# Retuned scheduling preferences in the mixing of a hybrid RWKV-7 and attention layer

## The chip, the cores and the metric

The kernel runs on one core of a Trainium2 chip. A core has five engines with instruction queues of their own: TensorE (PE, matrix products), VectorE (DVE), ScalarE (ACT), GpSimd (POOL) and SyncE (SP), which here does nothing but issue DMAs. Each engine works through its instructions strictly in order; across engines they wait for each other by semaphores. The metric is the time of one execution on the device, in microseconds.

## The reference

One layer of a streaming encoder, for 16 meta tokens, 512 tokens of a prompt and 64 tokens of a sample (592 rows of 1024 values):

```python
x += 1/2 * SwiGLU_a(RMSNorm(x))
p  = RMSNorm(x) @ w_in              # RWKV: r, k, v, decay, a, gate;  MLA: q-latent, kv-latent, rope-key
o_rwkv = RWKV-7 time mixing         # 8 heads of 64, a state per head, delta rule per token
o_mla  = latent attention           # 8 heads, causal by chunks of 64
x += concat(o_rwkv, o_mla) @ w_out
x += 1/2 * SwiGLU_b(RMSNorm(x))     # d_ff 2816
y  = RMSNorm(x)
```

RWKV's recurrence, per head and token, is `S = S*w + (S @ -kk) * kka + v * k` and `y = S @ r`. The kernel computes it in chunks of 64 tokens, for which a unit triangular system has to be solved in each chunk. Everything is float32; the large products are formed from split operands in three passes.

## The kernel before

The time has three stages: the first feed-forward network (to about 400 us), the mixing (to about 890 us), and the second feed-forward network. The change concerns the mixing.

**Units of RWKV.** `rwkv_unit(i, h, s)` treats head pair i (0 to 3) and half h of the tokens (0, 1): unit `3_0` is pair 3, first half. It is a generator with pauses (`yield`). Its first part prepares the chunk's operands and ends with the matrix `am` (L761), whose lower triangles go to DRAM as `ud` (four stores, L773) and come back as `up` (four loads, L777) with another layout. The second part turns operands by transposes (`tp`, `tb`, L791 and L792). Then comes the *solve*: `qm` is loaded with unit rows (L825), and 31 pairs of operations on POOL, `tt` (L830) and `qm` (L832), 62 steps in all, eliminate one column after the other; the result is stored as `qd` (L834) and read back into `qt` (four loads, L838). All of these DMAs are issued by SP (`RQ = nc.sync`). The rest of the unit forms the chunk's state products (`xb` L851 and L860, `tw` L875, `mps` L896, `sp` L918, `yp` L938 and on).

**Attention.** `attention(i)` treats two heads (pair i): keys and values from the latent (`kp` L1077, `vp` L1087), queries (`qp`, L1101), then nine blocks: four query tiles t of 128 rows for each of two heads hh, and one of the sample. `P_2_1_0` is pair 2, tile 1, head 0. For a block, scores `s` (L1155) go to PSUM, `softmax` fills the tile P, whose padding behind the last key is first set to zero by POOL (L1110; P has two buffers), and PE transposes P in blocks of 128 keys (`ptp`, L1134). The last of these blocks contains the zeroed columns. The products with the values are `ao` (L1186), and they go to DRAM as `od` (L985) or straight into the operands of the output product `wo` (L161 to L163).

**What sets the order.** The program is written as units and attention steps in turn (the loop at the end of the functions below). A scheduler then puts the instructions of each engine in an order by priorities and its own estimate of times. `later(what)` shifts the priority of everything that is issued inside it by `PRIORITY[what]` (or by the entry of the name's first part, such as `F2` for `F2_1`). `ATTENTION[n] = (before, during, after)` says how many steps of attention are issued ahead of, between and behind the later parts of unit n. So both tables hold numbers alone, and both decide in which place of each engine's queue an instruction stands.

Of the kernel before, what the change touches and what calls it, by code (L numbers as in the profile page):

```python
# [35 lines left out]
BANK_ORDER = ("C", "A", "D", "A", "D", "D", "B", "C")  # L36


PRIORITY = {"B": -1300, "S": -1600, "F2": -2400, "F1": -1300, "att": 1100, "w": 19300, "W": -500, "S_3": -3100,
# [6 lines left out]
ATTENTION = ((10, 0, 5), (11, 0, 4), (13, 0, 5), (13, 0, 7), (15, 0, 4), (12, 0, 7), (8, 0, 1), (11, 1, 13))  # L46


START = {"f1": "0aaaaaaa0aaa0babbbbbb0bbbb000110011t1t1121t212t222222", "f2": "aa0aaaaaba0ba1bb0babb0babb00b001101t1t1121t212t222222"}
# [31 lines left out]
def build(ctx: ExitStack, tc: tile.TileContext, I, O):  # L81
# [492 lines left out]
    @contextmanager  # L574
    def later(what):

        p, d = tc.cur_priority, PRIORITY.get(what, PRIORITY.get(what.split("_")[0], 0))
        tc.cur_priority = p + d
        yield
        tc.cur_priority -= d  # L580
# [619 lines left out]
    for n in range(8):  # L1200
        before, during, after = ATTENTION[n]
        with later(f"S_{n}"):
# [163 lines left out]
```

## Time and profile before

| | |
|---|---|
| median of 3 runs | 1304.87 us (1303.28 to 1307.77) |
| profiled execution | 1302.65 us |
| its span, first to last instruction | 1300.5 us |
| mean granted clock of PE | 0.983 |
| PE busy | 1259.3 us, 97% of the span |
| DVE, ACT, POOL busy | 990.7, 597.0, 545.0 us |

The profiled execution is one execution of its own, 2.22 us below the median; the times of rows come from it. A granted clock of 1.00 means 2.4 GHz, 0.50 means 1.2 GHz. In a timeline, a row gives the start, the duration (of all instructions of the row, where "x4" stands behind it), the engine, the line, and what was written from what; in brackets, how long the engine had been idle and what it waited for. SPq rows are DMA issues: the time is that of issuing, not of the transfer.

### The profile page before, as it was taken

What the parts mean: (1) busy time and instruction counts of PE and PEld (TensorE: products, weight loads), DVE (VectorE), ACT (ScalarE), POOL (GpSimd) and SP (SyncE); (2) the same over time, 40 slices, a digit from 0 to 9 for tenths busy, and PEclk for the clock granted to TensorE, in tenths of its full rate; (3) what the DMA queues carried; (4) which work ended last, traced back from release to release, by engine and by line L of the source; (5) the groups of instructions that cost most, each with busy time, mean ns of one, the idle gap of its engine ahead of it and who ended that gap; (6) DMA issues with size and microseconds to landing.
All of it is one profiled execution on the core that took longest, in us unless ns stands there. A gap on an engine that the chain in (4) does not pass through costs nothing. (4 is left out here: it accounts for less than half of the span.)

```text
span 1300.5 us, 26629 instructions
## 1 busy us (share of the span) xinstructions
PE 1259.3 (97%) x10104; PEld 1172.7 (90%) x10104; DVE 990.7 (76%) x2044; ACT 597.0 (46%) x1326; POOL 545.0 (42%) x811
## 2 busy tenths in 40 slices
PE   8999999999999999999999999998999999999997
PEld 7999999999999988877776667888999999999997
DVE  7876979888886654667677765578967989898974
ACT  7442434343444555554564545446533434343442
POOL 2333637464671006464562663000013736374760
PEclk9999999999999998989998989999999999999999
DMA  8222232323103422212113111134222222323112
GB/s 288 81 83 73 80 103 71 98 85 110 41 22 123 137 82 66 69 49 61 42 49 114 40 38 49 32 116 147 99 74 74 95 84 82 104 76 98 49 35 73
DMA packets 84255, 107.02 MB, mean 82 GB/s; under 512 B 24160, under 2 KB 44832, under 8 KB 84128
## 3 DMA queue, kind: packets, MB, share of 16 engines
q1 hardware_dynamic: 84128, 105.33, 26.3%
q8 instruction: 80, 1.31, 0.4%
q14 instruction: 47, 0.39, 0.1%
HBM read 96.78 MB, written 8.52 MB: 81 GB/s over the span
## 5 line engine op out<-in xcount | busy, mean ns | idle before, releaser
L830 POOL TENSOR_TENSOR tt<-qm,up 80x60 f32<-80x60 f32 (+24 forms) x248 | 84.9, 343 | 49.3 <-DMA up<-ud 21.3
L832 POOL TENSOR_TENSOR qm<-qm,tt 80x60 f32<-80x60 f32 (+24 forms) x248 | 84.0, 339 | 18.5
L1110 POOL MEMSET P<- 128x112 f32 (+1 forms) x36 | 6.8, 192 | 126.9 <-PE ptp L1134 87.6
L461 DVE SCALAR_TENSOR_TENSOR x<-f2o,x 128x288 f32<-128x288 f32 x88 | 38.7, 453 | 25.9 <-PE f2o L163 25.9
L461 DVE SCALAR_TENSOR_TENSOR x<-f1o,x 128x296 f32<-128x296 f32 x88 | 39.5, 461 | 23.6 <-PE f1o L163 23.5
L137 POOL TENSOR_TENSOR n_ops<-n,n_ops 128x296 fp32r<-128x296 f32 (+1 forms) x8 | 7.6, 948 | 90.9 <-DMA f_3A<-in_w13b 67.6
L161 PE MATMUL wo<-o,wo_h 128*128 128x288 f32 x128 | 41.2, 328 | 2.0 <-DVE x L1017 1.3
L162 PE MATMUL wo<-o,wo_h 128*128 128x288 f32 x128 | 39.8, 312 | 0.0
L163 PE MATMUL wo<-o,wo_l 128*128 128x288 f32 x128 | 38.0, 299 | 0.0
L136 ACT CAST f1w_h<-f1w_r 128x512 fp32r<-128x512 f32 x32 | 19.5, 617 | 21.8 <-PE f1o L162 19.8
L161 PEld LDWEIGHTS wo<-o,wo_h 128*128 128x128 f32 x128 | 24.0, 189 | 5.3 <-DVE x L1017 2.5
L1155 PE MATMUL s<-keys,qh 128*128 128x264 f32 (+3 forms) x80 | 27.9, 444 | 0.9 <-ACT pt L1140 0.5
L136 ACT CAST f2w_h<-f2w_r 128x512 fp32r<-128x512 f32 x32 | 19.2, 616 | 18.7 <-PE f2o L162 16.7
L761 DVE TENSOR_TENSOR am<-ab,cst 128x512 f32<-128x512 f32 (+1 forms) x32 | 15.0, 484 | 16.6 <-PE ab L757 16.5
L1134 PE MATMUL ptp<-ident,P 128*128 128x128 f32 (+1 forms) x128 | 23.2, 292 | 3.7 <-DVE P L1124 1.5
L1017 DVE TENSOR_TENSOR x<-wo,x 128x288 f32<-128x288 f32 x48 | 21.7, 454 | 6.7 <-PE wo L163 6.3
L1118 ACT ACTIVATE P<-s,m 128x264 f32<-128x264 f32 (+3 forms) x40 | 19.2, 483 | 15.9 <-DVE m L1116 15.6
L162 PEld LDWEIGHTS wo<-o,wo_h 128*128 128x128 f32 x128 | 24.3, 190 | 1.3 <-issue 0.7
L1134 PEld LDWEIGHTS ptp<-ident,P 128*128 128x128 f32 (+1 forms) x128 | 15.0, 144 | 11.1 <-issue 4.3
L163 PEld LDWEIGHTS wo<-o,wo_l 128*128 128x128 f32 x128 | 24.2, 189 | 0.8
L137 DVE TENSOR_TENSOR f1w_l<-f1w_r,f1w_h 128x512 fp32r<-128x512 f32 x32 | 24.0, 751 | 1.1 <-ACT f1w_h L136 0.2
L716 POOL MEMSET e<- 128x5 f32 x8 | 0.8, 106 | 56.9 <-DVE bk L765 56.9
(1261 smaller groups left out, 5677.0 us busy)
## 6 DMA issues: line engine op xcount, KB each, us to landing
f1w_r<-in_w2a SPq DMA_DIRECT2D x40, 256.0 KB
f2w_r<-in_w2b SPq DMA_DIRECT2D x40, 256.0 KB
wo_r<-in_w_out SPq DMA_DIRECT2D x12, 256.0 KB
up<-ud SPq DMA_DIRECT2D x32, 80.0 KB
x<-in_xT SPq DMA_DIRECT2D x8, 296.0 KB
xd<-x SPq DMA_DIRECT2D x2, 1184.0 KB
x<-xd SPq DMA_DIRECT2D x2, 1152.0 KB
f_1A<-in_w13a SPq DMA_DIRECT2D x4, 512.0 KB
```

What stands on the lines that cost most here:

```text
L136: S.copy(dst_hi, src)
L137: sub.tensor_tensor(dst_lo, src, dst_hi.bitcast(F32), ALU.subtract)
L161: T.matmul(out, wh, xh, start=i == 0, stop=False)
L162: T.matmul(out, wh, xl, start=False, stop=False)
L163: T.matmul(out, wl, xh, start=False, stop=i == n - 1)
L461: V.scalar_tensor_tensor(x[h][:, m], o[:, :n], 0.5, x[h][:, m], ALU.mult, ALU.add)
L830: G.tensor_tensor(t3, qm[:, :nj, st:st + 1].to_broadcast([4 * NP, nj, w]), up[:, st:st + 1, st + 1:].to_broadcast([4 * NP, nj, w]), ALU.mult)
L832: G.tensor_tensor(qm[:, :nj, st + 1:], qm[:, :nj, st + 1:], t3, ALU.subtract)
L1017: V.tensor_tensor(x2s[h][:, m], ps[:, :n], x2s[h][:, m], ALU.add)
L1118: S.activation(P[:, p0:p0 + n], s[:, :n], AF.Exp, bias=m[:, 2:3], scale=SCALE, accum_out=m[:, 4 + j:5 + j])
L1134: T.transpose(tp[:an, 128 * k:128 * k + 128], P[:, a0:a0 + an], ident)
L1155: T.matmul(s[:, :an], Q[:, hh, q0:q0 + 128], K[:, hh, a0:a0 + an], start=True, stop=True)
```

## The change

Numbers in the two tables change, and five names get an entry of their own. The same instructions are issued; the engines' queues differ between 574 us and 892 us of the trace of before, and are the same ahead of and behind that. In the changed kernel every line stands one further down, since the table has one line more.

```diff
-PRIORITY = {"B": -1300, "S": -1600, "F2": -2400, ...
+PRIORITY = {"B": -1300, "S": -1600, "F2": -2000, ...
...
-            "F1_7": -300, "W_k3": -800, "F2_7": -2600, "F1_0": -1200, "B_6": -1500, "W_k1": 700}
-ATTENTION = ((10, 0, 5), (11, 0, 4), (13, 0, 5), (13, 0, 7), (15, 0, 4), (12, 0, 7), (8, 0, 1), (11, 1, 13))
+            "F1_7": -300, "W_k3": -800, "F2_7": -2600, "F1_0": -1200, "B_6": -1500, "W_k1": 700, "F2_1": -4000,
+            "att_3": 200, "B_7": -2500, "B_4": -100, "S_5": -1200}
+ATTENTION = ((10, 0, 5), (11, 0, 4), (13, 0, 7), (13, 0, 8), (15, 0, 4), (12, 0, 8), (8, 0, 1), (11, 1, 13))
```

**SP, where unit 2_1's solve ends and unit 3_0's begins.** Before, the queue holds (`ud` and `up` feed the solve of 3_0, `qd` and `qt1` carry the result of 2_1; `wq3` are weights of attention):

```order
L773 DMA ud_3_0_9221<-am_3_0_9201 32x5x32 x4
L834 DMA qd_2_1_9659<-qm_2_1_9564 80x8x32
L1097 DMA wq3_0_10091<-in_wq 128x256
L777 DMA up_3_0_9226<-ud_3_0_9221 20x1024 x4
L838 DMA qt1_5279<-qd_2_1_9659 32x5x32 x4
L825 DMA qm_3_0_10437<-in_rows 80x256
```

In the changed kernel:

```order
L986 DMA od_5255<-ot_5_384_8816 128x128
L835 DMA qd_2_1_9692<-qm_2_1_9597 80x8x32
L986 DMA od_5255<-xn_1_1_8945 128x320
L839 DMA qt1_5279<-qd_2_1_9692 32x5x32 x4
L826 DMA qm_3_0_10460<-in_rows 80x256
L986 DMA od_5255<-ot_5_512_9041 128x64
L774 DMA ud_3_0_9247<-am_3_0_9227 32x5x32 x4
L778 DMA up_3_0_9252<-ud_3_0_9247 20x1024 x4
```

The store `qd` and the loads `qt1` of unit 2_1 have moved ahead of `ud` and `up` of unit 3_0, and so has one store of attention.

**POOL, at the start of unit 3_0's solve.** Before, from the last steps of unit 2_1's solve on:

```order
L832 TENSOR_TENSOR qm_2_1_9564<-qm_2_1_9564,tt_2_1_29_9653 80x8x2
L830 TENSOR_TENSOR tt_2_1_30_9656<-qm_2_1_9564,up_2_1_8421 80x8
L832 TENSOR_TENSOR qm_2_1_9564<-qm_2_1_9564,tt_2_1_30_9656 80x8
L716 MEMSET e_3_1_9678 128x5
L1110 MEMSET P_2_1_0_9314 128x112
L1110 MEMSET P_2_1_1_9332 128x112
L830 TENSOR_TENSOR tt_3_0_0_10439<-qm_3_0_10437,up_3_0_9226 80x31
L832 TENSOR_TENSOR qm_3_0_10437<-qm_3_0_10437,tt_3_0_0_10439 80x31
L830 TENSOR_TENSOR tt_3_0_1_10442<-qm_3_0_10437,up_3_0_9226 80x30
```

In the changed kernel, from the fourth step of unit 3_0's solve on:

```order
L833 TENSOR_TENSOR qm_3_0_10460<-qm_3_0_10460,tt_3_0_1_10465 80x30
L831 TENSOR_TENSOR tt_3_0_2_10468<-qm_3_0_10460,up_3_0_9252 80x29
L833 TENSOR_TENSOR qm_3_0_10460<-qm_3_0_10460,tt_3_0_2_10468 80x29
L831 TENSOR_TENSOR tt_3_0_3_10471<-qm_3_0_10460,up_3_0_9252 80x28
L833 TENSOR_TENSOR qm_3_0_10460<-qm_3_0_10460,tt_3_0_3_10471 80x28
L831 TENSOR_TENSOR tt_3_0_4_10474<-qm_3_0_10460,up_3_0_9252 80x54
L833 TENSOR_TENSOR qm_3_0_10460<-qm_3_0_10460,tt_3_0_4_10474 80x2x27
L831 TENSOR_TENSOR tt_3_0_5_10477<-qm_3_0_10460,up_3_0_9252 80x52
L833 TENSOR_TENSOR qm_3_0_10460<-qm_3_0_10460,tt_3_0_5_10477 80x2x26
L1111 MEMSET P_2_1_0_9314 128x112
```

The zeroing of P_2_1_0 has moved from in front of the solve to behind its twelfth step. That of P_2_1_1 follows after the twentieth. The transposes `ptp` of P_2_1_0 stand at the same place of PE's work in both kernels.

**PE, where attention pair 3 and the output product begin.** Before (`kp` and `vp` are keys and values of pair 3, `wo_0_1` and `wo_0_0` parts of the output product):

```order
L1077 MATMUL kp_3_424_10073<-cT_5631,w_uk_3_10065 128x424
L1087 MATMUL vp_3_0_10078<-w_uv_3_10066,cT_5631 128x128 x4
L161 MATMUL wo_0_1_0_10185<-o0_10132,wo_0_0_h_10166 128x288
L162 MATMUL wo_0_1_0_10185<-o0_10132,wo_0_0_h_10166 128x288
L163 MATMUL wo_0_1_0_10185<-o0_10132,wo_0_0_l_10167 128x288
L1087 MATMUL vp_3_4_10084<-w_uv_3_10066,cT_5631 128x128 x2
L1087 MATMUL vp_3_4_10084<-w_uv_3_10066,cT_5631 80x128
L634 MATMUL yp_2_1_9977<-acc_2_1_10012,cst_5262 128x320
```

In the changed kernel `kp_3_424` stands six rows ahead of these:

```order
L162 MATMUL wo_0_0_0_10194<-o0_10155,wo_0_0_h_10189 128x288
L792 MATMUL tp_3_0_4_10057<-ident_67,rkv_3_0_9183 128x128
L793 MATMUL tp_3_0_4_10057<-ident_67,bk_3_0_9184 128x128
L163 MATMUL wo_0_0_0_10194<-o0_10155,wo_0_0_h_10189 128x288
L164 MATMUL wo_0_0_0_10194<-o0_10155,wo_0_0_l_10190 128x288
L809 MATMUL av_3_0_10065<-zt_3_0_10040,am_3_0_9227 64x64 x8
L625 MATMUL yp_2_1_9996<-acc_2_1_10021,cst_5262 10x64 x5
L818 MATMUL gb_3_0_10079<-sga_5265,w_g2_3_8520 128x320
L809 MATMUL av_3_0_10065<-zt_3_0_10040,am_3_0_9227 64x64 x2
L1088 MATMUL vp_3_4_10084<-w_uv_3_9873,cT_5631 128x128 x2
L1088 MATMUL vp_3_4_10084<-w_uv_3_9873,cT_5631 80x128
```

The second part of the values, `vp_3_4`, has moved away from `kp_3_424`, and the products `wo_0` and the transposes of unit 3_0 stand between them.

## Rows read from the trace of the kernel before

**Rows 1.** the page: busy time, share and instructions of each engine:
```profile
PE 1259.3 (97%) x10104; PEld 1172.7 (90%) x10104; DVE 990.7 (76%) x2044; ACT 597.0 (46%) x1326; POOL 545.0 (42%) x811
```

**Rows 2.** table of windows: length; busy PE, PEld, DVE, ACT, POOL (count); clock, DMA share, GB/s:
```profile
574.00:892.00 318.00, 302.79 (x3026) 237.55 (x3027) 221.11 (x689) 169.90 (x459) 125.08 (x400) 0.97 0.24 69
```

**Rows 3.** PE's waits from 574 to 892 us: total, times, longest:
```profile
PE wo L161 <- DVE x L1017: 1.3, 1, 1.3
...
PE tp L791 <- ACT zt L801: 1.2, 2, 0.8
...
PE vp L1087 <- ACT keys L1079: 1.1, 1, 1.1
...
PE wo L161 <- ACT o L136: 0.7, 1, 0.7
```

**Rows 4.** timeline of POOL, 735 to 745 us: start, duration, what, idle before:
```profile
735.28 0.19 POOL L1110 MEMSET P<- 128x112 f32 x1 [4.45 <-PE ptp L1134]
...
737.55 0.23 POOL L830 TENSOR_TENSOR tt<-qm,up 80x31 f32<-80x31 f32 x1 [1.40 <-DMA qm<-in_rows]
...
742.03 0.27 POOL L830 TENSOR_TENSOR tt<-qm,up 80x50 f32<-80x50 f32 x1
...
744.86 0.31 POOL L832 TENSOR_TENSOR qm<-qm,tt 80x66 f32<-80x66 f32 x1
```

**Rows 5.** timeline of PE: transposes of P_2_1_0, then of P_2_1_1:
```profile
741.02 0.55 PE L1134 MATMUL ptp<-ident,P 128*128 128x128 f32 x3
...
744.82 0.38 PE L1134 MATMUL ptp<-ident,P 128*128 128x128 f32 x2
```

**Rows 6.** timeline of SP's DMA issues, 726 to 738 us:
```profile
727.04 1.77 SPq L773 DMA_DIRECT2D ud<-am  x4
730.83 0.30 SPq L834 DMA_DIRECT2D qd<-qm  x1
...
731.89 1.66 SPq L777 DMA_DIRECT2D up<-ud  x4
733.60 1.84 SPq L838 DMA_DIRECT2D qt<-qd  x4
735.49 0.43 SPq L825 DMA_DIRECT2D qm<-in_rows  x1
```

**Rows 7.** timeline of SP: unit 2_0's ud, up, qd and qt; unit 2_1's ud and up:
```profile
640.81 1.81 SPq L773 DMA_DIRECT2D ud<-am  x4
643.90 1.41 SPq L777 DMA_DIRECT2D up<-ud  x4
...
674.50 0.34 SPq L834 DMA_DIRECT2D qd<-qm  x1
676.45 1.77 SPq L838 DMA_DIRECT2D qt<-qd  x4
...
692.36 2.04 SPq L773 DMA_DIRECT2D ud<-am  x4
699.25 1.60 SPq L777 DMA_DIRECT2D up<-ud  x4
```

**Rows 8.** timeline of POOL: first step of the solve behind up at 643.90:
```profile
647.78 0.23 POOL L830 TENSOR_TENSOR tt<-qm,up 80x31 f32<-80x31 f32 x1 [5.45 <-DMA up<-ud]
```

**Rows 9.** windows around three half-speed stretches; columns as in rows 2:
```profile
693.47:696.88 3.41, 1.75 (x39) 1.52 (x40) 2.14 (x14) 3.27 (x12) 0.01 (x1) 1.00 1.09 360
696.88:703.71 6.83, 6.83 (x70) 4.93 (x68) 3.00 (x9) 0.97 (x5) 0.59 (x3) 0.50 0.35 92
...
754.90:765.14 10.24, 9.86 (x78) 7.22 (x78) 6.50 (x20) 2.95 (x11) 5.54 (x21) 0.50 0.21 48
...
789.04:792.45 3.41, 3.41 (x10) 2.54 (x8) 2.43 (x6) 1.29 (x4) 2.63 (x11) 0.50 0.31 91
```

**Rows 10.** timelines of SP and PE: unit 3_0's qd, and its first xb:
```profile
762.65 0.30 SPq L834 DMA_DIRECT2D qd<-qm  x1
...
792.66 0.50 PE L851 MATMUL xb<-q,am 32*32 32x32 f32 x20
```

More of the change, by code (lines that the diff above doesn't have):

```diff
@@ L36 @@
 BANK_ORDER = ("C", "A", "D", "A", "D", "D", "B", "C")
-PRIORITY = {"B": -1300, "S": -1600, "F2": -2400, "F1": -1300, "att": 1100, "w": 19300, "W": -500, "S_3": -3100,
[6 rows of a table removed]
-ATTENTION = ((10, 0, 5), (11, 0, 4), (13, 0, 5), (13, 0, 7), (15, 0, 4), (12, 0, 7), (8, 0, 1), (11, 1, 13))
+PRIORITY = {"B": -1300, "S": -1600, "F2": -2000, "F1": -1300, "att": 1100, "w": 19300, "W": -500, "S_3": -3100,
[7 rows of a table added]
+ATTENTION = ((10, 0, 5), (11, 0, 4), (13, 0, 7), (13, 0, 8), (15, 0, 4), (12, 0, 8), (8, 0, 1), (11, 1, 13))
 START = {"f1": "0aaaaaaa0aaa0babbbbbb0bbbb000110011t1t1121t212t222222", "f2": "aa0aaaaaba0ba1bb0babb0babb00b001101t1t1121t212t222222"}
```

10 rows, old and new, of the table PRIORITY are left out of this document.

## The prediction

> **What bounds the kernel now.** I read the page first. TensorE (PE) is busy 97% of the span [rows 1]; so time is lost only where PE waits, or where its clock is halved. The order of every engine is the same in both kernels up to 574 us and from 892 us on, so the change acts only in the 318 us of the mixing between them. The table of windows says that PE is busy 302.79 us of these at a mean clock of 0.97 [rows 2]: 15.2 us of idle time is all that a better order could win there, apart from the clock. The list of PE's waits in that stretch shows this idle time as some thirty listed waits of 0.2 to 1.3 us; rows 3 are the ones that the argument needs [rows 3]. No single one carries the kernel; what a new order can do to the end is to take some of them away, or to make a long one.
>
> For a long one I looked at what runs beside PE with little room. GpSimd (POOL) works through the triangular solve of one RWKV unit in 62 steps, in order, and between them zeroes the padding of attention's P tiles. The solve of unit 3_0 starts at 737.55, and the P tile of block 1_0 of attention pair 2 (P_2_1_0) is zeroed ahead of it, at 735.28 [rows 4]. PE transposes this tile with the row at 741.02 [rows 5], so the zeroing has 6 us to spare before the change. SyncE (SP) issues every DMA in order; the loads and stores that feed the solve stand in its queue [rows 6].
>
> **The change part by part.** It moves instructions and neither adds nor removes one, so engine time is the same and only waits count.
>
> 1. *The zeroing of P.* In the changed kernel P_2_1_0 is zeroed after 12 steps of the solve of 3_0 instead of before the solve. PE's transposes of that tile stand at the same place in PE's work as before. So PE now waits for the start of this solve, plus 12 steps. The first 12 steps took from 737.55 to 742.03, 4.48 us, and the zeroing 0.19 us [rows 4].
>
> 2. *The start of that solve.* Before, SP issues the four stores ud of unit 3_0 at 727.04, ahead of the store qd of unit 2_1, which waits on SP until the solve of 2_1 is done: it is issued at 730.83 [rows 6]. After, qd stands first, then the four qt loads that wait for qd to land, qm, one od store, and only then ud and up of 3_0. Behind the waiting qd everything on SP is held. With the end of 2_1's solve where it was, the chain is: qd 730.83; qt 1.95 us after qd, as at 674.50 to 676.45 [rows 7], so 732.78; four qt in 1.77 us [rows 7], 734.55; qm in 0.43 us [rows 6] and an od store, taken as long, 735.4; up can be issued 3.09 us after the first ud when nothing else is in the way (640.81 to 643.90), and the solve starts 3.88 us after the first up (643.90 to 647.78) [rows 7, 8]: 742.4. That is 4.9 us later than 737.55.
>
> 3. *The wait on PE.* 742.4 + 4.48 + 0.19 gives 747.1 for the end of the zeroing. The block that needs it is the last of the three transposes at 741.02 (0.55 us for the three) [rows 5], so it began near 741.3: PE stands 5.8 us later at this point. Since 747.1 comes from POOL and SP, small waits won or lost on PE earlier than that do not count; they only make the wait itself longer or shorter. The same holds for other zeroings that stand deeper in a solve (P_1_4_0 after 35 steps of the solve of 2_1 instead of 13): they bind, if at all, before this point. P_2_1_1 is zeroed after 20 steps of the solve of 3_0. Its last transpose came near 745.0, 3.7 us after that of P_2_1_0 [rows 5]; the eight steps between took from 742.03 to 745.17 [rows 4], 3.1 us, and another zeroing 0.2, so it just fits and is no second wait.
>
> The ends of this cost: the only term with a wide spread is the time from ud to up. Unit 2_1 took 6.89 us for it (692.36 to 699.25) behind large transfers, against 3.09 [rows 7]. If the wait in unit 3_0 is as long, PE loses 9.6 us. If unit 2_1's own is as short this time, its solve and all behind it come 3.8 us earlier, and 2.0 us are left. I take 5.8, because between 727 and 745 SP's queue holds only small transfers, like the 3.09 row.
>
> 4. *Small waits behind that point.* Gone are the wait of vp on the keys (1.1 us), since kp and vp of pair 3 now stand some 4 us of PE work apart, and that of wo on the split of o (0.7 us) [rows 3]. In return three places stand closer to what they wait for: the second transposes of unit 3_0, the sample step's scores of pair 2, and the scores of block 3_0 of pair 3 behind the last wo of the first four. None has a wait of its own in before; each lies between 0 and the longest of the list, 1.3 us [rows 3]. I take 1.0 us for the three together. Net 0.8 us won; ends: 1.8 won to 2.1 lost.
>
> 5. *The tail from 860 us.* The wo products and their evictions change places among themselves; order and amount of work on PE behind them stay. Taken at 0, with ±0.5 us.
>
> The solve of 3_0 itself may end late: its qd was issued at 762.65, and PE's first use of the result, the row of xb, came at 792.66 [rows 10]; 30 us cover the 4.9. The solve of 3_1 starts behind it and ends later too; I take the same cover for it, and 1 to 2 us if it fails.
>
> Sum: 5.8 − 0.8 = 5.0 us. The profiled execution took 1302.65 us for a span of 1300.5 us; with the change 1307.65. It lies 2.22 us under the median of the runs, 1304.87, so the forecast in terms of the median is 1309.9 us.
>
> **Clock.** At 696.88 the granted clock falls to the lower level (0.50, that is 1.2 GHz) for 6.83 us, after 3.41 us in which PE was busy for only 1.75; the stretches at 754.90 and 789.04 are of the same kind, with 10.24 and 3.41 us [rows 9]. A stretch of this kind costs at most half its length, 1.7 to 5.1 us. Behind a wait of 5.8 us I expect one, at about 747; but before already has the one at 754.90, which I expect to be the same one moved, and that at 789.04 may go with the wait on vp in front of it. So the sum holds 0 for the clock, with ends of 5.1 us lost and 1.7 us won. The Trainium skill, TensorE: Matmul & The Clock Gate, section "HAM oscillation — how this bites in real kernels", says that waits between pieces of matmul work throttle the array so that the next piece starts at half rate; the trace agrees at 696.88. By this rule the wait of step 3 is paid for twice, and the third rival below is what it would make of the time.
>
> **The rivals.**
>
> *Faster: PE is never held.* The solve of 2_1 ends some 6 us earlier, so that P_2_1_0 is zeroed before 741. For it: 3.8 us of this are there if ud to up of unit 2_1 falls from 6.89 to 3.09, and its loads follow work on PE from which small waits go (tp on zt, two of 1.2 us together [rows 3]). Against it: the two large loads that are in the way are released by the same matmul as before. Then PE keeps about 2 us of the small waits before 741, the 0.8 of step 4, and up to 1.7 of the stretch at 789.04: 4.5 us won, 1300.4 us. It decides from a solve of 3_0 that starts at 736.5 or sooner.
>
> *No change: the place on SP costs only its issue time.* Then the solve of 3_0 starts later by the four ud and the od that are issued between, 1.77 and 0.43 us, thus at 739.8; the zeroing ends at 744.4, PE is held 3.1 us, and with step 4 the time is 1307.2 us; with unit 2_1's shorter path 1306.1. For it: in before the same ud waited 4.85 us for their up, only because other DMAs stood between [rows 6]; part of that chain is slack. Against it: qd itself waits for the end of the solve, and ud comes behind it. The Trainium skill, DMA: Bandwidth & Descriptors, section "Issuing engines are not separate DMA queues", has this as its rule: the engine that issues matters for the sequencer's time alone, which is usually small beside the transfer. The rows of unit 2_1 and 3_0 show waits in the queue, not issue time, as the larger part; I follow the rows.
>
> *Slower still.* All of the forecast, and a half-speed stretch in addition, as long as that at 754.90: 5.1 us more, 1315.0 us.
>
> **How the numbers follow.** The forecast has 0.36, slower still 0.14, no change 0.27, faster 0.23. A measurement of this kernel tells about 0.3% (3.9 us) from no change. The first two are slower by more than that: 0.50; same 0.27; faster 0.23. The forecast's own range is 1306.1 (a wait of 2.0) to 1313.7 us (9.6). The range that should hold 8 of 10 reaches from 1300 (most of the faster case) to 1315 us.
>
> **What would show it.** In the profile after, the first step of unit 3_0's solve at 742 instead of 737.55; SP with qd and qt ahead of ud there; a memset of P at about 747 after 12 steps of it; and on PE a wait of ptp on POOL of some 4 to 6 us, the longest in the mixing, which leaves later work 5 us late. The waits of vp on the keys and of the first wo on o are gone. The forecast is wrong if that ptp wait is under 2 us, or if PE's later work has caught up by 800 us; the clock's part is wrong if the half-speed stretches between 690 and 892 us sum to well under or over the 20.5 us of before.

## The result, and the profile after

| | before | after |
|---|---|---|
| median | 1305.52 us of 4 runs (1303.28 to 1307.77) | 1319.06 us of 4 runs (1317.30 to 1324.87) |
| profiled execution, its span | 1302.65, 1300.5 us | 1319.48, 1317.7 us |
| mean granted clock | 0.983 | 0.977 |

The ratio is 1.0107, with an interval of 1.0080 to 1.0134: 14 us slower where 5 were forecast. In after every line stands one further down than in before.

```profile
PE 1269.8 (96%) x10104; PEld 1178.2 (89%) x10104; DVE 991.2 (75%) x2044; ACT 596.1 (45%) x1326; POOL 541.9 (41%) x811
```

This is the row of busy time of after. The other engines' work is the same within 3.1 us; PE is busy 10.5 us longer than in [rows 1] (matmuls at half speed last longer); the span grew by 17.2 us. So in this execution some two fifths are waits and the rest is in matmuls that took longer.

Most of what the forecast was built on did happen. First SP's queue, in the timeline of after (start, duration of the issue, line):

```profile
731.86 0.34 SPq L835 DMA_DIRECT2D qd<-qm  x1
...
733.87 1.77 SPq L839 DMA_DIRECT2D qt<-qd  x4
735.69 0.43 SPq L826 DMA_DIRECT2D qm<-in_rows  x1
...
736.64 2.04 SPq L774 DMA_DIRECT2D ud<-am  x4
740.67 1.41 SPq L778 DMA_DIRECT2D up<-ud  x4
```

`ud` of unit 3_0 stands behind qd and qt, and is issued at 736.64 instead of 727.04 [rows 6]. Then POOL, at the start of that solve and at the zeroing of P_2_1_0, and PE's transposes of this tile:

```profile
745.73 0.27 POOL L831 TENSOR_TENSOR tt<-qm,up 80x31 f32<-80x31 f32 x1 [13.79 <-DMA up<-ud]
...
749.94 0.19 POOL L1111 MEMSET P<- 128x112 f32 x1
...
750.18 0.48 PE L1135 MATMUL ptp<-ident,P 128*128 128x128 f32 x1 [2.68 <-POOL P L1111]
```

The solve starts at 745.73 (forecast 742.4; before 737.55 [rows 4]), the zeroing comes at 749.94 (forecast 747.1), and PE waits for it. But it waits for 2.68 us, not 5.8: at 747.50 it had come to this place 6.2 us later than before (741.3). The waits of PE around it (total, number, longest), from 700 to 790 us:

```profile
PE ptp L1135 <- POOL P L1111: 2.7, 1, 2.7
PE ao L1187 <- ACT P L1119: 1.9, 1, 1.9
PE ptp L1135 <- DVE P L1125: 1.3, 2, 0.8
PE sp L919 <- DVE gt L903: 1.0, 1, 1.0
PE av L809 <- ACT zt L802: 0.9, 1, 0.9
...
PE yp L635 <- DVE acc L632: 0.8, 1, 0.8
```

Before, over the same work (699 to 778 us), had no wait on POOL and none over 0.8 us. The wait on POOL is the longest of the list, and by itself a fifth of the loss. To see where the rest lies I cut PE's work into seven stretches of before, and in the other traces at the same count of PE's matmuls. "At half speed" is how long the granted clock was 0.50 over this work; at most half of that time is lost. The last two columns are two of the experiments below.

| PE's work, by before's time | before | after | after, once more (e1) | middle alone (e13) | ties and tail undone (e6) |
|---|---|---|---|---|---|
| 574 to 648 | 73.97 | 78.19 | 78.38 | 73.96 | 78.22 |
| 648 to 705 | 56.92 | 53.34 | 53.22 | 57.04 | 53.18 |
| 705 to 742 | 37.13 | 45.44 | 45.29 | 40.75 | 42.08 |
| 742 to 776 | 33.89 | 36.62 | 38.01 | 37.81 | 37.88 |
| 776 to 810 | 33.95 | 31.72 | 32.08 | 31.72 | 31.94 |
| 810 to 852 | 42.05 | 44.99 | 45.29 | 44.35 | 44.17 |
| 852 to 905 | 52.96 | 56.18 | 57.05 | 53.88 | 53.09 |
| sum | 330.87 | 346.48 | 349.33 | 339.51 | 340.57 |
| at half speed | 20.5 | 30.7 | 37.6 | 17.1 | 23.9 |

After loses 8.3 us between 705 and 742, 3.2 to 4.1 in the tail from 852, 2.9 to 3.2 between 810 and 852, 2.7 to 4.1 between 742 and 776 and 4.2 ahead of 648; it wins 3.6 between 648 and 705 and 1.9 to 2.2 between 776 and 810. The cut at 705 lies where the two orders differ, so the two rows beside it are safest together: 4.7 us lost between 648 and 742. The wait of vp on the keys [rows 3] is gone as forecast. That of wo on o is not; before's and then after's row of it:

```profile
799.76 0.40 PE L161 MATMUL wo<-o,wo_h 128*128 128x288 f32 x1 [0.72 <-ACT o L136]
...
809.87 0.40 PE L162 MATMUL wo<-o,wo_h 128*128 128x288 f32 x1 [0.77 <-ACT o L137]
```

The 4.2 us ahead of 648 are one half-speed stretch. The windows of after on both sides of its start (length; busy PE, PEld, DVE, ACT, POOL with counts; clock, DMA share, GB/s):

```profile
629.60:633.01 3.41, 2.27 (x24) 1.50 (x24) 1.83 (x6) 2.31 (x7) 2.86 (x12) 1.00 0.05 15
633.01:643.25 10.24, 10.24 (x46) 7.36 (x46) 3.74 (x8) 2.83 (x7) 2.26 (x10) 0.50 0.21 47
...
749.06:759.30 10.24, 8.89 (x46) 5.24 (x46) 4.72 (x19) 2.51 (x8) 8.58 (x30) 0.50 0.00 1
```

And the same piece of work in before, where the clock stayed at 1.00:

```profile
629.30:632.71 3.41, 2.26 (x24) 1.50 (x24) 1.82 (x6) 2.31 (x6) 2.86 (x12) 1.00 0.06 16
```

In the 3.41 us ahead of 633 PE's busy time is the same to 0.01 us in both; one execution fell, the other did not. In the tail the wait of wo on x was 1.3 us in before [rows 3] and that of f_0c 1.2; those on o and on P were not there. PE's waits of after from 852 to 905:

```profile
PE wo L162 <- DVE x L1018: 2.2, 1, 2.2
PE f_0c L162 <- ACT n L274: 1.3, 1, 1.3
PE wo L162 <- ACT o L137: 1.2, 1, 1.2
PE ao L1187 <- ACT P L1119: 0.9, 1, 0.9
```

### The profile page after: what moved, and what is told of

It is laid out like the page before. It is cut to its first block, busy times and chain, and to the rows that moved or that the text cites. A ratio compares the mean times of both kernels' runs of the same rounds, so it can differ in the third digit from the quotient of the medians.

```text
span 1317.7 us, 26645 instructions
## 1 busy us (share of the span) xinstructions
PE 1269.8 (96%) x10104; PEld 1178.2 (89%) x10104; DVE 991.2 (75%) x2044; ACT 596.1 (45%) x1326; POOL 541.9 (41%) x811
## 5 line engine op out<-in xcount | busy, mean ns | idle before, releaser
L162 PEld LDWEIGHTS wo<-o,wo_h 128*128 128x128 f32 x128 | 23.6, 188 | 7.7 <-DVE x L1018 3.2
L1187 PE MATMUL ao<-pt,vt 128*64 128x128 f32 x224 | 25.6, 310 | 4.7 <-ACT P L1119 2.8
L1187 PEld LDWEIGHTS ao<-pt,vt 128*64 128x64 f32 x224 | 16.2, 150 | 12.3 <-ACT P L1119 4.1
L1141 DVE COPY pt<-ptp 128x384 f32<-128x384 f32 (+3 forms) x36 | 17.8, 494 | 9.6 <-PE ptp L1135 9.2
```

The source lines that it names most:

```text
L162: T.matmul(out, wh, xh, start=i == 0, stop=False)
L1187: T.matmul(op[rows, :128], vt[:, k, rows], pts[hh][:, k], start=k == 0, stop=k == t + 1)
```

## The experiments

An order can be held without touching a table: a function chains each engine's instructions in the sequence of a list, which adds no wait between engines. The kernels below (but e1) are one of the two with such a list; "at 705" is a place in PE's work by before's time, and on the other engines what starts there.

```diff
         build(tc, I, O)
+        hold_order(tc)
```

Each was timed beside runs of before on its chip. Holding an order costs nothing that shows: e8, e12 and e14 hold one too and lie within 0.3% of before.

| | median us, runs | ratio to before, interval |
|---|---|---|
| e1 after, once more | 1319.66, 4 | 1.0098, 1.0069 to 1.0127 |
| e2 after, the hold of P_2_1_0 undone | 1320.30, 4 | 1.0104, 1.0077 to 1.0130 |
| e3 after, the tail as before | 1317.66, 4 | 1.0086, 1.0058 to 1.0114 |
| e4 after, the head as before | 1318.06, 4 | 1.0089, 1.0066 to 1.0113 |
| e5 after, three ties undone | 1314.02, 4 | 1.0080, 1.0052 to 1.0108 |
| e6 e5 and the tail as before | 1309.55, 10 | 1.0038, 1.0016 to 1.0059 |
| e7 before, POOL's order of after | 1307.62, 10 | 1.0017, 0.9998 to 1.0036 |
| e8 before, the head of after | 1302.82, 10 | 0.9998, 0.9973 to 1.0023 |
| e9 before, 704 to 819 of after | 1316.92, 6 | 1.0101, 1.0078 to 1.0125 |
| e10 before, the tail of after | 1308.80, 12 | 1.0035, 1.0017 to 1.0053 |
| e11 before, VectorE's q_2_1 of after | 1308.85, 12 | 1.0030, 1.0013 to 1.0047 |
| e12 before, 648 to 705 of after | 1303.22, 12 | 0.9986, 0.9964 to 1.0008 |
| e13 before, 704 to 852 of after | 1316.39, 6 | 1.0078, 1.0055 to 1.0101 |
| e14 e12 once more | 1303.81, 12 | 0.9990, 0.9973 to 1.0007 |

**e1, e2: is it the wait on POOL?** e1 is after without an edit. In e2 the two moves are undone on which the forecast rests:

```diff
 SP:    od (attention)
+       ud_3_0 x4
        qd_2_1, od
+       up_3_0 x4
        qt_2_1 x4, qm_3_0, od
-       ud_3_0 x4, up_3_0 x4
 POOL:  last step of the solve of 2_1
+       zeroing of P_2_1_0, P_2_1_1
        first step of the solve of 3_0 ...
-       (zeroing behind its steps 12 and 20)
```

> The changed kernel itself once more, for a second trace. In the first trace the clock of TensorE fell to half at 633.01 for 10.24 us and cost 4.8 us, behind waits that stand in the trace of before as well (1.14 against 1.15 us), where it did not fall. If that half-speed stretch belongs to the new order, it stands here again within 1 us of the same place, and the time is 13 to 14 us over before. If it is chance of one execution, it is missing, the span is 4 to 5 us shorter than 1317.7, and before shows it in some executions too.

> The changed kernel with two moves taken back, every other order held as it was: on SP the four ud stand ahead of qd of unit 2_1 and the four up ahead of the qt loads, on POOL the zeroing of P_2_1_0 and P_2_1_1 ahead of the solve of unit 3_0. My theory (the hold of TensorE at 747 to 750 costs what the lag between 741 and 800 us grew by): the wait of ptp on POOL (2.7 us) is gone, the time falls by 3.5 to 5 us, to about 1314.5. Rival 1 (the hold only takes the place of other waits, or the half-speed stretch at 749 comes anyway and is what costs): it falls by less than 1.5 us. Rival 2 (the late solve of 3_0 delays all that follows, the tail included): it falls by 8 us or more, and the waits of wo on o and x near 886 and 900 are gone.

e1 repeats the loss, and the wait on POOL (2.8 us). e2 is no faster than after (1320.30), where 3.5 to 5 us were expected; the intervals leave room for some 4 us either way. Its wait on POOL is gone from PE; these stand there instead, PE's waits and then DVE's:

```profile
PE ptp L1134 <- DVE P L1124: 3.3, 2, 2.8
PE yp L634 <- DVE acc L631: 2.7, 1, 2.7
...
DVE q L845 <- PE xb L875: 3.1, 1, 3.1
DVE P L1124 <- POOL P L1110: 2.0, 1, 2.0
```

So taking away the forecast's wait gave nothing back that shows. Both of these waits lie ahead of it in PE's work, and both come through DVE. First, DVE waits for the zeroing of another tile (P_1_4_0, which after places behind 35 steps of the solve of 2_1 instead of 13). In after PE had lost 4 us in the stretch at 633 and came later to this place; this execution of e2 had no such stretch, and neither had those of e3 and e4 below, where DVE waits 1.6 us here. Second, DVE waits with five transposes `q`, which after has moved ahead of a block's softmax, for `qt`, the result of that solve. (The row names xb; `qt` is what the transposes read, and e11 below names it.) The edit itself makes this second wait, since it puts ud and up ahead of qd and qt again. In after, where SP issues qd and qt first, the transposes do not wait, nor do they in e1, e3, e4, e9 and e13:

```profile
736.83 0.58 DVE L846 STREAM_TRANSPOSE q<-qt 128x32 f32<-128x32 f32 x5
```

I call these places *ties*: an engine that has its own work to do stands in order behind something that comes out of POOL's solve. That the forecast's wait is worth nothing by itself e2 does not show, as it puts another in its place.

**e3, e4: the two ends.** The order of before behind 852, and the order of before up to 662:

```diff
 every engine, e3:
-after
+after up to 852, before behind it
 every engine, e4:
-after
+before up to 662, after behind it
```

> The changed kernel up to 864 us, and from there on each engine in the order of before (66 rows of TensorE differ). My theory (the tail's order costs 2.5 to 4 us, since wo of the last pair now stands 2.4 instead of 3.3 us behind the matmul whose result its operand is split from, and the evictions behind it on VectorE are late): the wait of 1.2 us of wo on o and most of the 2.2 us of wo on x are gone, the time falls by 2.5 to 4 us. Rival (the tail is late only because work comes late from the hold): no change within 1 us.

> The changed kernel, but in the order of before up to 662 us (22 rows of TensorE differ, all of them ahead of the stretch at 633). If the half-speed stretch at 633 is set off by the new order ahead of it: it is gone and the time falls by 4 to 5 us. If it is a matter of chance or of small shifts in time: no steady change (0 to 1 us in the median), and the stretch may stand here too or be missing in single traces.

Both are 1 to 2 us under after, within their intervals of it (2.5 to 4 were expected of e3). Neither has the wait of ptp on POOL in its trace, and both keep most of the loss: PE came to that place too late by other ways. In e4 the stretch at 633 did not come, so 574 to 648 took 73.98 us as in before; but 705 to 742 then took 49.19, with one half-speed stretch of 17.07 us. The loss sits in the middle, and time won ahead of it is lost there.

**e5 to e7: the ties.** e5 is e2 with POOL's whole order of before, and

```diff
 DVE:   qh (attention's queries)
-       q_2_1 x5 (reads qt, the result of the solve)
        softmax of blocks P_2_0_0 and P_2_0_1
+       q_2_1 x5
```

e6 is e5 with the tail as before. e7 is before with POOL's order of after:

```diff
 POOL:  steps of the solve of 2_1
-       zeroing of P_1_4_0 behind step 13
+       zeroing of P_1_4_0 behind step 35
        ... (the zeroings behind it later as well)
```

> After, with three ties to GpSimd's solve of unit 2_1 undone: GpSimd's own order is that of before (P_1_4_0, P_2_1_0 and their neighbours are zeroed early in the solves), SP issues ud and up of unit 3_0 ahead of qd and qt, and VectorE takes its five transposes q2_2_1 behind its scaling of P_2_0_1 as before. Ties theory: the waits of VectorE on GpSimd's P near 717 (1.6 to 2.0 us), of TensorE for acc (2.3 to 2.7 us) and of the transposes ptp on P go, the stretch 705 to 742 of before falls from 45 to 49 us to some 38 to 40, and the time falls by 4 to 8 us to 1311 to 1315. Rival (each tie only replaces another, or the clock decides): within 1.5 us of after, 1317.5 to 1320.5.

> The kernel with the three ties undone, and besides every engine in the order of before from 864 on. Ties theory with the tail's two late evictions and feeds as a separate cost: 2 to 4 us less than the three ties alone, 1308 to 1312. Rival (the tail costs nothing of its own): within 1 us of the three ties undone.

> Before, with GpSimd's order alone taken from after: the zeroing of P_1_4_0 and P_2_1_0 stands deeper in the solves, nothing else is moved. Ties theory: VectorE is held some 4 us at P_1_4_0 near 717 to 721, TensorE then waits over 2 us for acc, and P_2_1_0 comes about 1 us late; with at most one more half-speed stretch the time is 3 to 8 us over before, 1308.5 to 1313.5. Rival (hidden, since VectorE has slack there): within 1.5 us of before.

e5 and e6 came within the theory's ranges of time: 5 us for the ties by the medians, though e5's interval overlaps that of after, and 4.5 us more for the tail (2 to 4 were expected). The clean pair is e3 against e6, which differ in the three ties alone: 1.0086 and 1.0038, 6 us (some 2 to 11 by the two intervals). Which of the three carries it is not shown; in e3's trace only that of P_1_4_0 is a wait. The clock has a large part in it. (1 − clock) × span is the most that half speed can have cost a run, and by the granted clocks of all runs its mean is 33 us in e3, 23 in e6 and 24 to 25 in before. In e3's trace PE waits 2.3 us for acc behind the tie, and a half-speed stretch of 13.65 us begins at 718.38.

e7's trace shows the tie of P_1_4_0 by itself; its timeline of POOL, and the scaling of that tile on DVE:

```profile
720.13 0.20 POOL L1110 MEMSET P<- 128x128 f32 x1
...
720.36 0.50 DVE L1124 TENSOR_SCALAR P<-P,m 128x464 f32<-128x464 f32 x1 [2.48 <-POOL P L1110]
```

Before had the zeroing at 708.89 and this row with no wait:

```profile
708.89 0.20 POOL L1110 MEMSET P<- 128x128 f32 x1 [0.85 <-PE ptp L1134]
...
716.92 0.45 DVE L1124 TENSOR_SCALAR P<-P,m 128x464 f32<-128x464 f32 x1
```

DVE stands 2.5 us, and 705 to 742 takes 44.49 us instead of 37.13, 10.24 of it at half speed. But the next stretch is 1.7 shorter, and the timed price is 2.2 us (−0.3 to 4.7): between the two theories, not settled by itself.

**e11: the tie of q_2_1 by itself.** Before, with the five transposes moved as after has them (the diff above, read the other way).

> Before, with VectorE's five transposes of q_2_1, which read the solve's result qt, ahead of block 2_0's softmax instead of behind its scaling of P_2_0_1; nothing else is moved. Ties theory: VectorE stands near 735 to 737 until qt has landed and TensorE's ptp of block 2_0 waits for P: 0.5 to 3 us over before, 1305.5 to 1308. Rival (qt is there in time, or VectorE has slack): within 0.5 us of before.

3.9 us (1.7 to 6.1), above the theory's range; the clock has no part in it (24 us by the estimate above, as in before). In its timeline of DVE

```profile
736.70 0.58 DVE L845 STREAM_TRANSPOSE q<-qt 128x32 f32<-128x32 f32 x5 [3.77 <-DMA qt<-qd]
```

and in its list of PE's waits from 735 to 745

```profile
PE ptp L1134 <- DVE m L1122: 4.9, 1, 4.9
```

The transposes run at 736.70; in before they ran at 736.55, behind the softmax:

```profile
736.55 0.58 DVE L845 STREAM_TRANSPOSE q<-qt 128x32 f32<-128x32 f32 x5 [0.23 <-DMA qt<-qd]
```

So they gain nothing from the earlier place. Only the softmax now stands behind them, and PE's transposes wait 4.9 us for it. This is the plainest price of one move in the study. But it is the price on before's order: in after, by the row above, the same transposes find `qt` there.

**e8 to e10, e13: head, middle and tail apart.**

```diff
 every engine of before:
 e8:  +order of after up to 705
 e9:  +order of after from 704 to 819
 e10: +order of after from 852 on
 e13: +order of after from 704 to 852
```

> Every engine in the order of after up to 705 of before's profile, and in that of before behind it. Ties theory: the loss sits behind 705, so the time is that of before or up to 3.7 us less (no half-speed stretch near 697), 1302 to 1306. Rival (the lag is prepared earlier, by the order of the head, and only shows behind 705): 4 us or more over before, 1309.5 and up.

> Before, with the order of after on every engine from 704 of before's profile to 819 alone. Theory (the loss is made between 705 and 776 by the order there, whatever stands ahead or behind): 8 to 11 us lost in 705 to 776, 2 won back in 776 to 810, so 6 to 10 us over before, 1311 to 1315. Rival (it needs the later start that the head of after brings, or shows only with the tail): within 3 us of before.

> Before, with the order of after on every engine from 852 on alone: the eviction of o and the feed x come later, the half of wo that uses o stands 2.4 instead of 3.3 us behind yp_3_1. Theory (the tail has a cost of its own): wo waits over 1 us for o and over 2 us for x, 3 to 5 us over before, 1308 to 1310. Rival (these waits come of the lag made ahead of them): within 1.5 us of before.

> Before, with the order of after on every engine from 704 to 852 of before's profile, so that the middle stands alone and the place where the two orders meet behind it is the one of the tail's comparison, not one inside unit 3_0 as in e9. Theory (head about nothing, middle and tail add up to the whole loss): 7 to 10 us over before, 1312 to 1315, and the stretch 810 to 852 back at 42 to 44 us. Rival (the middle alone is worth all of the loss, and the tail's cost overlaps with it): 12 us or more over before, 1317 and up.

The head costs nothing (−0.3 us, −3.5 to 3.0). The tail alone costs 4.6 us (2.2 to 6.9); its waits are those of after:

```profile
PE wo L161 <- DVE x L1017: 1.7, 1, 1.7
PE f_0c L161 <- ACT n L273: 1.4, 1, 1.4
PE wo L161 <- ACT o L136: 1.2, 1, 1.2
```

e9 missed its range: 13.2 us. By its trace it lost 5 us up to 810 and some 8 more near 818, where its two orders meet inside unit 3_0, in waits of 0.7 to 1.5 us and a fall of the clock; that part belongs to neither kernel. e13 meets at 852 instead, and there 810 to 852 takes 44.35 us (after 44.99). Its price is 10.2 us (7.2 to 13.2); the theory had 7 to 10, the rival 12 or more, and the interval holds both, so only the estimate lies nearer to the theory. Head, middle and tail sum to 14.5 us; after has 14.0 (10.4 to 17.5). PE's waits of e13 from 742 to 790:

```profile
PE mps L896 <- DVE zt L881: 3.6, 1, 3.6
PE ao L1186 <- ACT P L1118: 1.9, 1, 1.9
PE ptp L1134 <- POOL P L1110: 1.2, 1, 1.2
PE av L808 <- ACT zt L801: 0.9, 1, 0.9
```

Before's longest there is 0.5 us. The 3.6 us are a fourth tie, which e5 and e6 leave in place. DVE in before, then in e13:

```profile
766.84 0.86 DVE L881 COPY zt<-tw 64x256 f32<-64x256 f32 x2 [0.44 <-ACT w L878]
...
769.70 0.57 DVE L845 STREAM_TRANSPOSE q<-qt 128x32 f32<-128x32 f32 x5
...
773.47 0.58 DVE L845 STREAM_TRANSPOSE q<-qt 128x32 f32<-128x32 f32 x5 [3.58 <-DMA up<-ud]
...
774.21 0.84 DVE L881 COPY zt<-tw 64x256 f32<-64x256 f32 x2
```

These transposes read the result of unit 3_0's solve. The new order has them ahead of the copies `zt` on which PE's mps waits, instead of behind, and the later solve of 3_0 reaches PE by this way. (The row names up; e6, below, names qt.) In after, which came to this place later, the wait of mps is 0.2 us.

The middle's loss does not need the clock: e13's profiled execution had less time at half speed than before's (17.1 against 20.5 us), and its work took 8.6 us longer by the table. But it was the fastest of six. The other five had granted clocks of 0.975 to 0.979 against its 0.982, and by the estimate above half speed has some 4 of the 10.2 us.

With the ties and the tail undone, e6 is still 5.0 us over before (2.1 to 7.7; its profiled execution, 1316.09 us, is 6.5 over its median, so its column in the table is an unfavourable example). Its waits from 742 to 790, and DVE's row behind the second:

```profile
PE ao L1186 <- ACT P L1118: 1.9, 1, 1.9
PE mps L896 <- DVE zt L881: 1.4, 1, 1.4
PE av L808 <- ACT zt L801: 0.9, 1, 0.9
...
780.26 0.58 DVE L845 STREAM_TRANSPOSE q<-qt 128x32 f32<-128x32 f32 x5 [2.44 <-DMA qt<-qd]
```

ao follows a softmax more closely than in before, and mps waits by the fourth tie. No run took these moves away one by one, so that they make up the last 5 us is argued from the trace, not shown.

**e12, e14: a better version?** After won 3.6 us between 648 and 705, where before has the fall of 696.88 [rows 9].

```diff
 every engine of before:
+order of after from 648 to 705
```

> Before, with the order of after on every engine from 648 of before's profile to 705 alone, where after needed 53.3 us for the work that took before 56.9. Theory (the order of this stretch keeps TensorE at full speed where it fell near 697): 2 to 4 us less than before, 1301 to 1303. Rival (which stretch falls to half speed is not set by the order there, and the fall comes elsewhere): within 1 us of before.

> The kernel of e12 once more (before, with after's order from 648 to 705 alone), to narrow its interval. Theory (that order keeps TensorE at full speed near 697): 1.5 to 3.5 us less than before, and over both calls an interval below 1. Rival (its falls to half speed only come elsewhere): within 1 us of before.

Two times −1.3 to −1.8 us, and both intervals span 1: no version here is shown to beat before. In both profiled executions the stretch itself took 52.7 us instead of 56.9. But one execution had no fall between 574 and 742 and a span of 1295.7 us; the other fell at 635.73 and took 1308.6. A single profile of this kernel would have told either story.

## Why the prediction was wrong

**Its direction was right and the wait that it named was there, but the loss is 14 us and not 5, and most of it lies in places that it put at nothing or did not price.** By its steps:

1. *Steps 1 and 2* (zeroing behind 12 steps; SP's queue). Right in kind. The start of the solve was 3.3 us later than forecast: qd was 1.0 us late, `up` came 4.03 us behind `ud` instead of 3.09, and the first step 5.06 behind `up` instead of 3.88. The Trainium skill, DMA: Bandwidth & Descriptors, section "Issuing engines are not separate DMA queues", has the issuing engine matter for its sequencer's time alone; here `ud` moved by 9.6 us, while the issues put ahead of it (qd, two od, qt, qm) take 3.4, so the waits in the queue decided, as the prediction chose.
2. *Step 3 failed.* "Since 747.1 comes from POOL and SP, small waits won or lost on PE earlier than that do not count." PE did go on when POOL let it, 8.9 us later than before instead of 5.8, since the zeroing was 3.0 us later than forecast. But 6.2 of the 8.9 us it had lost by then, and where it lost them in other ways (e3, e4) it did not wait on POOL at all and the kernel lost 11 to 12 us even so. So the loss does not hang on this wait. The second sentence that failed names the right tile: P_1_4_0's zeroing "binds, if at all, before this point". I looked whether PE reads the tile in time, and not whether DVE, which scales all of it, stands behind the zeroing with all its other work. e7 shows DVE standing 2.5 us there.
3. *Two moves were not priced at all:* the transposes of q_2_1 ahead of a softmax on DVE, and those of q_3_0 ahead of zt. The first costs 3.9 us on before's order (e11) and is no wait in after's traces. For the second, the prediction counted 30 us from the solve of 3_0 to PE's xb at 792.66 [rows 10]; but DVE reads the result at 769.70 already, 7 us behind the qd of 762.65, and e13 shows 3.6 us of PE behind it.
4. *Step 4.* Of the two waits that it took away, that of vp (1.1 us) is gone and that of wo on o stayed (0.77 us); the stretch 776 to 810 is 2.2 us shorter, but before also had its half-speed stretch of 789.04 there. What stands closer was priced at 1.0 us for three places by the longest wait in before; new ones of 1.9, 1.3, 1.0 and 0.9 us came, and what e6 still loses (5.0) lies mostly between 705 and 776.
5. *Step 5.* 0 ± 0.5 for the tail; it is 4.6 us (e10). I counted PE's work behind it as unchanged and did not see that the half of wo which uses o stands closer to the last yp (3.4 us of PE's work from start to start instead of 4.7), and that the evictions on DVE and ACT that release it moved with it.
6. *Clock.* Taken at 0, with +5.1 as the end. Behind 690 us that held in the profiled execution: after's half-speed stretches there, at 708.10, 749.06, 772.96 and 902.66, sum to 20.5 us as in before. Over all its work after was at half speed for 10.2 us more than before (17.1 in e1), which in after is the stretch near 633. By the granted clocks of all runs (0.977 in the mean of eight executions of after, 0.981 in the seven of before beside e1) half speed has some 5 of the 14 us, as an estimate, and waits the rest. Some of it follows waits: a stretch of 10.24 us begins at 749.06, inside the wait on POOL. There the trace agrees with the Trainium skill, TensorE: Matmul & The Clock Gate, section "HAM oscillation — how this bites in real kernels", which has PE pay for a wait a second time. But the stretch near 633 is not set by the order alone: it came in after, e1, e5, e6, e8 and in e10 and e14, whose order there is before's, and not in before, e2 to e4, e7, e9, e11 to e13. That is 5 of 7 executions with after's order there and 2 of 9 with before's; whether the order makes it more likely is not shown, and e8 finds no price of the head. So the third rival (all of the forecast and one more stretch, 1315.0) came near the time for a reason that is only part of it.

The test that the prediction set for itself, a ptp wait of over 2 us, was passed (2.7), which shows how little one confirmed wait says: it was the last of several losses in a row, and the earlier ones had used up most of its price.

## What to carry to other kernels

When an order changes, list every instruction that moved ahead of something on an in-order engine, and ask of each what it waits for and what now stands behind it; the engine that pays may be a third one (POOL's zeroing held DVE, and DVE held PE). Several such ties to the same late producer can stand in for each other: undoing one may bring out the next, or make a new one. Undoing them together tells what they cost; adding one alone to the old order tells its price there, which need not be its price in the new order. And compare more than one execution before reading a clock stretch as an effect, or its absence as a proof.

## What was not expected of the hardware

Ahead of 633 PE had 24 matmuls and 2.27 and 2.26 us of busy time in 3.41 us in two executions, and was granted 0.50 for 10.24 us in one and 1.00 in the other. With before's order up to 704 in both, e10 fell there and e13 did not, and of e12 and e14, which are the same kernel, only e14 fell; the stretch costs about 4 to 5 us of PE's time (78.19 in after and 78.64 in e10 against 73.97), a third of the effect that was to be measured.
